# What follows on the experts' products is queued behind the cast, split and product of the chunk in front

## The chip, the core and the metric

The kernel runs on one core of one Trainium2 chip, as one launch. A core has TensorE for matrix products (PE in the profile, its weight loads PEld), VectorE (DVE), ScalarE (ACT) and GpSimd (POOL) for everything else, and SyncE (SP), which here issues most of the transfers. Each engine works through its own list of instructions in a fixed order and waits, where an instruction needs another engine's result or a buffer that is still in use, on a semaphore. The metric is the device time of one execution in microseconds. The times shown here are three runs and one profiled execution.

## The reference

One layer of an encoder on 512 tokens of 1024 numbers: a convolution module and a state-space mixer side by side, then a mixture of 32 experts of which each token takes 4, then a final norm. The change lies in the experts:

```python
gu = xb @ w_gu[e] + b_gu[e]                 # 1024 -> 2048
gate, up = jnp.split(gu, 2, axis=-1)
gate = jnp.minimum(gate, SWIGLU_LIMIT)
up = jnp.clip(up, -SWIGLU_LIMIT, SWIGLU_LIMIT)
glu = gate * jax.nn.sigmoid(SWIGLU_ALPHA * gate)
return ((up + 1.0) * glu) @ w_down[e] + b_down[e]   # 1024 -> 1024
...
out = jax.ops.segment_sum(ys * buf_w[:, None], buf_tok, num_segments=t + 1)[:t]
```

All numbers are float32. An expert's weights are 12 MB, and all 32 experts' are read once.

## The kernel before

The first 880 us or so compute the mixer, the convolution and the routing. From then on the experts follow one another in steps. A step has one block of tokens, up to 128 (a large expert, `three3`) or up to 64 (a small one, `two2`); from step 2 on large and small take turns, and two steps (11 and 21) have a second, small block for the same expert.

The weights come in **chunks** of 1 MB, 384 in all, numbered `n` in the order in which they are used: 8 for the gate and up product (`gu`, 128 of the 1024 rows each) and 4 for the down product (`dn`, 256 rows each). In most steps (`mixed`) the down chunks of the expert before are put between the gate and up chunks of this one. Every chunk goes through the same stations:

- SP loads it into one of `NRAW` = 7 raw buffers (`mr`, `m_load`).
- ScalarE casts it to fp32r, the high part (`mh`, line 1352), VectorE takes what the cast lost, the low part (`ml`, line 1353, the split); both are written by `m_split` into one of `NHL` = 4 slots. The raw buffer is free when the split is done.
- TensorE multiplies (`m_product`): with a large block 12 products of 512 columns a chunk (high by high, low by high, high by low), with a small one 8. The slots of `mh` and `ml` are free when they are done.

In the loop over chunks `m_load(n + 6)`, `m_split(n + 3)` and `m_product(n)` are written one after the other. On the products follow, by name:

- `lower` (ScalarE, `bgu` and `bdn`, line 1450) copies the lower 64 rows of a small block's result, which hold the products with the tokens' low part,, and `folded` (TensorE, line 1453) adds them to the upper 64; `bias` (line 1436) adds a large block's bias.
- `act`: ScalarE's `sg` (line 1415) and VectorE's two operations on `h` (1416, 1417).
- `h_parts`: TensorE transposes `h` (`trh`, line 1385), ScalarE and VectorE split it into `hh` and `hl` (1395, 1396); the down products read both.
- `leave`: VectorE scales the result into `y` (line 1427), and `scatter` adds it to the output with an indirect transfer of GpSimd (line 1431).
- `gather` (line 1366) fetches the next tokens with an indirect transfer, and `x_parts` transposes and splits them (`trx`, `xh`, `xl`; 1385, 1392, 1393).

For a small block some of this is put into the list `late`, which the loop works off behind the next chunk's product. The order of the instructions on an engine is not the order of this text: a scheduler lays them out when the kernel is built, by its own estimate of when each could start, and an instruction that it thinks ready early is put ahead of others that are written before it. `tc.issue_after(i)` is the means to bind it: instructions traced under it stay behind `i` on `i`'s engine.

After the last chunk come two loops that run only if an expert has more tokens than its blocks hold (here they are branched over), then the final norm, which reads the sum from `y_d`.

Of the kernel before, what the change touches and what calls it, by code (L numbers as in the profile page):

```python
# [2 lines left out]

# [5 lines left out]
F32 = mybir.dt.float32  # L9
# [12 lines left out]
D = 1024  # L22
KT = D // P
# [6 lines left out]
NE = 32  # L30
# [10 lines left out]
def encoder_layer_kernel(ctx: ExitStack, tc: tile.TileContext, a, out):  # L41
# [160 lines left out]
    for k in range(KT):  # L202
        pt = bank("mm", f"xT{k}")
# [1095 lines left out]
    def mixed(s):  # L1299

        return 0 < s < NE - 1 and len(steps[s]) == len(steps[s - 1]) == 1
# [41 lines left out]
    ms = mw2 = None  # L1343
    slot = {}

    def m_split(n):
        if n >= len(chunks):
            return
        raw = raws.pop(n)
        hi = mh.tile([P, 2 * DFF], F32R, tag="hi", bufs=NHL, name=f"mh{n}")  # L1350
        lo = mh.tile([P, 2 * DFF], F32R, tag="lo", bufs=NHL, name=f"ml{n}")
        S.copy(hi, raw)  # L1352
        V.tensor_sub(lo, raw, hi.bitcast(F32))  # L1353
        hls[n] = (hi, lo)

    order = [b for st_ in steps for b in st_]
# [42 lines left out]
    def x_parts(s):  # L1399
        if s < NE:  # L1400
            for b in steps[s]:
                if b in small:
                    slot[b]["fold"] = f_ = folds[small_at.index(b) % 2 if b < NE else 2]
                    G.tensor_copy(f_[:HB, :HB], selb[:, b:b + 1].bitcast(F32).to_broadcast([H2, HB]))  # L1404
                slot[b]["xT"] = two_parts(slot[b]["x"], "x", b)
# [3 lines left out]
    def act(b, gate, up, c0, n):  # L1409
        q, r = slot[b], rows(b)  # L1410
        if "h" not in q:
            q["h"] = ms.tile([P, DFF], F32, tag="hy", bufs=3, name=f"h{b}")[r]
        sg = ms.tile([P, DFF], F32, tag="sg", bufs=1, name=f"sg{b}")[r, c0:c0 + n]
        h = q["h"][:, c0:c0 + n]
        S.activation(sg, gate[r], AF.Silu, scale=ALPHA)
        V.tensor_scalar(h, up[r], LIMIT + 1.0, 1.0 - LIMIT, ALU.min, ALU.max)  # L1416
        V.scalar_tensor_tensor(h, sg, SILU_LIMIT, h, ALU.min, ALU.mult)
# [5 lines left out]
    def leave(b, cols, pd):  # L1423
        q, r = slot[b], rows(b)
        if "y" not in q:
            q["y"] = ms.tile([P, D], F32, tag="hy", bufs=3, name=f"y{b}")[r]
        V.scalar_tensor_tensor(q["y"][:, cols], pd[r], q["w"], tl["g2"][r, cols], ALU.mult, ALU.mult)  # L1427
# [10 lines left out]
    def three3(pt, l, r, k, w, cols, first):  # L1438
        PE.matmul(pt, l[:, k, :], w[0][:, cols], start=first, stop=False)  # L1439
        PE.matmul(pt, r[:, k, :], w[0][:, cols], start=False, stop=False)  # L1440
        PE.matmul(pt, l[:, k, :], w[1][:, cols], start=False, stop=False)  # L1441

    def two2(pt, l, k, w, cols, first):
        PE.matmul(pt, l[:, k, :], w[0][:, cols], start=first, stop=False)  # L1444
        PE.matmul(pt, l[:, k, :], w[1][:, cols], start=False, stop=(k == KT - 1))  # L1445

    def lower(pt, tab):
        S.copy(tab[HB:], pt[HB:])  # L1450
# [25 lines left out]
    def out_small(b, pt, cols, last):  # L1476
        for c0 in range(cols.start, cols.stop, T):
            folded(pt[:, c0 - cols.start:c0 - cols.start + T], b, bdn[:, c0:c0 + T])
            leave(b, slice(c0, c0 + T), pt[:, c0 - cols.start:c0 - cols.start + T])
        if last:  # L1480
            scatter(b)

    def m_product(n, kind, blocks, k):
        w = hls.pop(n)
        b = blocks[0]
        if kind == "gu" and len(blocks) == 1:
            if k == 0:
                pend["gu"] = [banks(f"gu{i}", b) for i in range(2)]
            gate, up = (flat(x) for x in pend["gu"])
            for j in range(4):  # L1490
                cs, pt = slice(j * T, (j + 1) * T), pend["gu"][j // 2][:, j % 2, :]
                parts(b, "xT", k, pt, w, cs, k == 0)
                if k == KT - 1 and b not in small:
                    bias(pt, b, bgu, cs)
            if k == KT - 1:
                if b in small:
                    lower(gate, bgu[:, 0:D])
                    lower(up, bgu[:, D:])
                    late.append(lambda: act_small(b, gate, up, None))
                else:  # L1500
                    act(b, gate, up, 0, D)
        elif kind == "gu":
            n_, kp = divmod(k, 4)
            if kp == 0:
                pend["gu"] = [banks(tag, b_) for tag, b_ in zip(("dn", "gu0") if n_ else ("gu0", "gu1"), blocks)]
            for kk in range(2):
                for i, b_ in enumerate(blocks):
                    for h in range(2):
                        cs = slice(kk * D + h * T, kk * D + (h + 1) * T)
                        parts(b_, "xT", 2 * kp + kk, pend["gu"][i][:, h, :], w, cs, kp == 0 and kk == 0)  # L1510
            if kp == 3:
                cols = slice(n_ * T, (n_ + 1) * T)
                (g1_, u1_), (g2_, u2_) = ([x[:, h, :] for h in range(2)] for x in pend["gu"])
                for h, pt in enumerate((g1_, u1_)):
                    bias(pt, b, bgu, slice(h * D + n_ * T, h * D + (n_ + 1) * T))
                act(b, g1_, u1_, n_ * T, T)
                for h, pt in enumerate((g2_, u2_)):
                    lower(pt, bgu[:, h * D + n_ * T:h * D + (n_ + 1) * T])
                late.append(lambda: act_small(blocks[1], g2_, u2_, cols))
        elif len(blocks) == 1:  # L1520
            if k == 0:
                pend["dn"] = banks("gu0" if b == NE - 1 else "dn", b)
            for kk in range(2):
                for j in range(2):
                    cs = slice(kk * D + j * T, kk * D + (j + 1) * T)
                    parts(b, "hT", 2 * k + kk, pend["dn"][:, j, :], w, cs, k == 0 and kk == 0)
            if k == 3:
                pt = flat(pend["dn"])
                if b in small:
                    lower(pt, bdn)  # L1530
                    out_small(b, pt, slice(0, D), True)
                else:
                    for j in range(2):
                        cs = slice(j * T, (j + 1) * T)
                        bias(pt[:, cs], b, bdn, cs)
                        leave(b, cs, pt[:, cs])
                    scatter(b)
        else:
            n_, kq = divmod(k, 2)
            if kq == 0:  # L1540
                pend["dn"] = banks("gu1" if n_ else "dn", b)
            for kk in range(4):
                for i, b_ in enumerate(blocks):
                    parts(b_, "hT", 4 * kq + kk, pend["dn"][:, i, :], w, slice(kk * T, (kk + 1) * T), kq == 0 and kk == 0)
            if kq == 1:
                cs, (p1_, p2_) = slice(n_ * T, (n_ + 1) * T), [pend["dn"][:, i, :] for i in range(2)]
                bias(p1_, b, bdn, cs)
                leave(b, cs, p1_)
                if n_:
                    scatter(b)  # L1550
                lower(p2_, bdn[:, cs])
                late.append(lambda: out_small(blocks[1], p2_, cs, n_ == 1))

    tlw.close()
    mw2 = moe.enter_context(tc.tile_pool(name="mw2", bufs=1, reuse_waits="tile"))
# [54 lines left out]
    for n, (kind, s, k) in enumerate(chunks):  # L1610
        if n:
            m_load(n + NRAW - 1)
        if n == 3 * KT:
            n_rest = nc.values_load(ovr[0:1, 2 * NOVR:2 * NOVR + 1], min_val=0, max_val=NOVR)
            n_any = nc.values_load(ovr[0:1, 2 * NOVR + 1:2 * NOVR + 2], min_val=0, max_val=1)
        if n == len(chunks) - 4:
            with tc.issue_after(last_load[0].ins):
                final_rows()
        m_split(n + NHL - 1)
        now, late[:] = list(late), []  # L1620
        m_product(n, kind, steps[s], k)
        for f_ in now:
            f_()
        if s == 0 and kind == "gu" and k < KT - 1:
            next(placing, None)
            if k >= KT - 1 - len(biases):
                bias_table(*biases[k - KT + 1 + len(biases)])
        if kind == "gu" and k == (4 if s == 0 else 6 if mixed(s) else KT - 1):
            x_parts(s + 1)
        if kind == "gu" and k == KT - 1:  # L1630
            gather(s + 2)
        if kind == "gu" and s > 0 and k == 1:
            h_parts(steps[s - 1])
        if kind == "dn" and s == NE - 2 and k == 3:
            h_parts(steps[s + 1])

    V.scalar_tensor_tensor(tl["gf"], tl["gf"], 1.0, tl["g_"], ALU.add, ALU.mult)


# [78 lines left out]
```

## Time and profile before

| | |
|---|---|
| runs | 2109.12, 2112.2, 2113.71 us; median 2112.2 |
| the profiled execution's own time | 2111.7 us |
| its span, first to last instruction | 2110.0 us |
| PE, PEld busy | 1908.0 us (90%), 1458.8 us (69%) |
| DVE, ACT, POOL busy | 1728.4 us (82%), 1336.9 us (63%), 686.5 us (33%) |
| DMA | 548.52 MB, mean 260 GB/s |
| a chunk's cast, a chunk's split | 1905 ns, 2282 ns, 384 of each |
| a 1 MB load, issue to landing | 7.7 us (median) |

Busy shares are a mean over parts of the kernel that have different limits; what matters here is the stretch from 950 us on, where the experts are. A busy TensorE is not one at its peak: a product that waits for an operand after it has begun counts as busy. "A <- B" in a row of waits means that the instruction A stood at the head of its engine's list and B ended its wait. Chunk numbers are not in the trace; they are in the orders of instructions shown with the change, as the number behind `mh`, `ml` and `mr`.

### The profile page before, as it was taken

To read this page: it belongs to the slowest core of one execution; us is meant where nothing else is said; L and a number is where in the kernel's file an instruction comes from. 1 tells how busy PE (TensorE), PEld (TensorE's weight loads), DVE (VectorE), ACT (ScalarE), POOL (GpSimd) and SP (SyncE) were. 2 spreads that over 40 slices of the span, in tenths; PEclk is the share of its full clock that TensorE was granted. 3 is DMA by queue.
4 is the path that set the end of the run, shared out by engine and by line. 5 is a ranking of instruction groups with operands and counts; after the bars stand their busy time and mean duration, and the time that the engine had idled before them with its cause. 6 is when DMAs were issued, how large, how long until landed. Compare 5 with 4: busy or idle time off the path is not lost.

```text
span 2110.0 us, 24644 instructions
## 1 busy us (share of the span) xinstructions
PE 1908.0 (90%) x8412; PEld 1458.8 (69%) x8412; DVE 1728.4 (82%) x1646; ACT 1336.9 (63%) x1556; POOL 686.5 (33%) x387
## 2 busy tenths in 40 slices
PE   5998999989997999799999899999989999989983
PEld 4776777767776778677667667776666777766662
DVE  7878888989857555699989887888988888898895
ACT  4657567576746223367677775776777677677773
POOL 2166364565654232321122132132212312321103
PEclk8999999999998999799999999999999999999996
DMA  8443313224366867589999999899999989999993
GB/s 265 120 138 94 89 55 85 72 64 123 102 203 192 265 207 248 175 313 384 360 360 371 371 336 352 325 350 366 354 364 351 345 319 348 367 353 351 356 374 131
DMA packets 232643, 548.52 MB, mean 260 GB/s; under 512 B 18006, under 2 KB 124766, under 8 KB 201789
## 3 DMA queue, kind: packets, MB, share of 16 engines
q1 hardware_dynamic: 224258, 529.01, 69.8%
q0 software_dynamic: 8208, 17.89, 3.7%
q8 instruction: 68, 1.11, 0.2%
q14 instruction: 61, 0.50, 0.1%
q10 hardware_dynamic: 48, 0.01, 0.0%
HBM read 526.37 MB, written 29.91 MB: 264 GB/s over the span
## 4 chain that ended last, share of the span: by engine, by line
PE 39%; DVE 11%; issue 8%; ACT 3%; DMA 1%; POOL 1%; another core or an unknown queue 0%; POOLq 0%; DVEq 0%; SPq 0%; ACTq 0%
DVE ml L1353 8%; PE gu L1439 6%; PE gu L1441 6%; PE gu L1440 5%; PE gu L1444 3%; PE gu L1445 3%; PE dn L1445 3%; PE dn L1441 2%; PE dn L1444 2%; PE dn L1440 2%; PE dn L1439 2%; ACT mh L1352 1%; PE gu L1436 1%; ACT bgu L1450 1%; DVE hl L1396 1%
## 5 line engine op out<-in xcount | busy, mean ns | idle before, releaser
L1353 DVE TENSOR_TENSOR ml<-mr,mh 128x2048 fp32r<-128x2048 f32 x384 | 861.9, 2282 | 71.6 <-ACT mh L1352 71.2
L1352 ACT CAST mh<-mr 128x2048 fp32r<-128x2048 f32 x384 | 711.9, 1905 | 95.2 <-PE gu L1444 41.9
L1431 POOL DMA_INDIRECT y_d<-y,toks_b x32 | 125.2, 3913 | 373.6 <-DVE y L1427 351.8
L1445 PE MATMUL gu<-ml,xh 128*128 128x512 f32 x576 | 215.4, 402 | 28.9 <-DVE ml L1353 27.7
L1444 PE MATMUL gu<-mh,xh 128*128 128x512 f32 x576 | 209.3, 392 | 0.0
L1439 PE MATMUL gu<-mh,xh 128*128 128x512 f32 x480 | 195.7, 408 | 1.2 <-ACT xh L1392 1.2
L1440 PE MATMUL gu<-mh,xl 128*128 128x512 f32 x480 | 189.6, 395 | 1.0 <-DVE xl L1393 1.0
L635 DVE SCALAR_TENSOR_TENSOR ha<-hb,c,ha 128x497 f32<-128x497 f32 (+14 forms) x240 | 176.8, 737 | 6.8 <-ACT ha L630 4.3
L1441 PE MATMUL gu<-ml,xh 128*128 128x512 f32 x480 | 181.8, 400 | 0.3 <-DVE ml L1353 0.2
L1366 POOL DMA_INDIRECT xg<-v_d,toks_b x32 | 116.2, 3630 | 187.2 <-PE trx L1385 180.6
L1445 PEld LDWEIGHTS gu<-ml,xh 128*128 128x128 f32 x576 | 108.1, 188 | 66.9 <-DVE ml L1353 45.2
L1404 POOL CAST fold<-selb 64x64 fp32r<-64x64 f32 x18 | 33.5, 1869 | 321.6 <-PE dn L1453 296.1
L1444 PEld LDWEIGHTS gu<-mh,xh 128*128 128x128 f32 x576 | 108.2, 188 | 21.0 <-issue 1.0
L1445 PE MATMUL dn<-ml,hh 128*128 128x512 f32 x256 | 104.8, 409 | 14.9 <-DVE ml L1353 14.9
L722 DVE SCALAR_TENSOR_TENSOR acc<-araw,cT,acc 128x512 f32<-128x512 f32 x84 | 83.3, 992 | 39.7 <-DMA araw<-in_final_ada_w_dram 22.4
L1441 PE MATMUL dn<-ml,hh 128*128 128x512 f32 x240 | 97.8, 408 | 17.8 <-DVE ml L1353 17.2
L1439 PEld LDWEIGHTS gu<-mh,xh 128*128 128x128 f32 x480 | 91.0, 190 | 30.6 <-issue 11.5
L1441 PEld LDWEIGHTS gu<-ml,xh 128*128 128x128 f32 x480 | 90.5, 190 | 23.8 <-issue 4.7
L1444 PE MATMUL dn<-mh,hh 128*128 128x512 f32 x256 | 103.9, 406 | 0.7 <-DVE h L1416 0.6
L1440 PEld LDWEIGHTS gu<-mh,xl 128*128 128x128 f32 x480 | 91.2, 190 | 19.0 <-DVE xl L1393 1.7
L1440 PE MATMUL dn<-mh,hl 128*128 128x512 f32 x240 | 93.9, 391 | 0.8 <-DVE hl L1396 0.8
L1439 PE MATMUL dn<-mh,hh 128*128 128x512 f32 x240 | 94.1, 392 | 0.0
(570 smaller groups left out, 4277.8 us busy)
## 6 DMA issues: line engine op xcount, KB each, us to landing
mr<-in_w_gu_dram SPq DMA_DIRECT2D x240, 1024.0 KB, 7.7
mr<-in_w_down_dram SPq DMA_DIRECT2D x128, 1024.0 KB, 7.8
araw<-in_ada_w_dram SPq DMA_DIRECT2D x64, 256.0 KB, 2.8
mr<-in_w_gu_dram SPq DMA_DIRECT2D x32, 512.0 KB, 9.1
ada<-in_ada_w_dram SPq DMA_DIRECT2D x32, 256.0 KB, 5.4
wX_raw<-in_w_in_dram SPq DMA_DIRECT2D x16, 512.0 KB, 3.9
wZ_raw<-in_w_in_dram SPq DMA_DIRECT2D x16, 512.0 KB, 3.8
araw<-in_final_ada_w_dram SPq DMA_DIRECT2D x32, 256.0 KB, 4.9
```

The source lines that it names most:

```text
L635: V.scalar_tensor_tensor(acc[:, lo_:hi_], h[:, lo_ + s:hi_ + s], c1[:, i, k:k + 1], acc[:, lo_:hi_], ALU.mult, ALU.add)
L722: V.scalar_tensor_tensor(acc, raw, cT[:, k:k + 1], acc, ALU.mult, ALU.add)
L1352: S.copy(hi, raw)
L1353: V.tensor_sub(lo, raw, hi.bitcast(F32))
L1366: gathered.append(nc.gpsimd.indirect_dma_start(out=x_, out_offset=None, in_=v_d, in_offset=bass.IndirectOffsetOnAxis(ap=tok_[r], axis=0), ...
L1404: G.tensor_copy(f_[:HB, :HB], selb[:, b:b + 1].bitcast(F32).to_broadcast([H2, HB]))
L1431: nc.gpsimd.indirect_dma_start(out=y_d, out_offset=bass.IndirectOffsetOnAxis(ap=q["tok"], axis=0), in_=q["y"], in_offset=None, bounds_chec ...
L1439: PE.matmul(pt, l[:, k, :], w[0][:, cols], start=first, stop=False)
L1440: PE.matmul(pt, r[:, k, :], w[0][:, cols], start=False, stop=False)
L1441: PE.matmul(pt, l[:, k, :], w[1][:, cols], start=False, stop=False)
L1444: PE.matmul(pt, l[:, k, :], w[0][:, cols], start=first, stop=False)
L1445: PE.matmul(pt, l[:, k, :], w[1][:, cols], start=False, stop=(k == KT - 1))
```

## The change

`m_split` and the products write down their last cast, split and matmul in `last_of`. The context `queued()` binds what is traced in it behind these three, each on its engine. Under it stand now: `lower` and `act` at the end of a gate and up product, `lower` and `leave` at the end of a down product, what `late` holds, and `x_parts`, `gather` and `h_parts` in the loop. GpSimd's and SP's instructions have no entry in `last_of`. Beside this `out_small` of a small expert's only block goes into `late` instead of being called at once; `out_small` of a two-block step's last half is called at once instead of going into `late`; and what is left in `late` after the loop is worked off there.

```diff
+    last_of = {}
+
+    @contextmanager
+    def queued():
+
+        with ExitStack() as st_:
+            for i in last_of.values():
+                st_.enter_context(tc.issue_after(i.ins))
+            yield
...
-        S.copy(hi, raw)
-        V.tensor_sub(lo, raw, hi.bitcast(F32))
+        last_of["ACT"] = S.copy(hi, raw)
+        last_of["DVE"] = V.tensor_sub(lo, raw, hi.bitcast(F32))
...
-        PE.matmul(pt, l[:, k, :], w[1][:, cols], start=False, stop=False)
+        last_of["PE"] = PE.matmul(pt, l[:, k, :], w[1][:, cols], start=False, stop=False)
...
-                    lower(gate, bgu[:, 0:D])
-                    lower(up, bgu[:, D:])
+                    with queued():
+                        lower(gate, bgu[:, 0:D])
+                        lower(up, bgu[:, D:])
                     late.append(lambda: act_small(b, gate, up, None))
                 else:
-                    act(b, gate, up, 0, D)
+                    with queued():
+                        act(b, gate, up, 0, D)
...
                 if b in small:
-                    lower(pt, bdn)
-                    out_small(b, pt, slice(0, D), True)
+                    with queued():
+                        lower(pt, bdn)
+                    late.append(lambda: out_small(b, pt, slice(0, D), True))
...
-                        leave(b, cs, pt[:, cs])
+                        with queued():
+                            leave(b, cs, pt[:, cs])
...
-                late.append(lambda: out_small(blocks[1], p2_, cs, n_ == 1))
+                if n_:
+                    out_small(blocks[1], p2_, cs, True)
+                else:
+                    late.append(lambda: out_small(blocks[1], p2_, cs, False))
...
         m_product(n, kind, steps[s], k)
-        for f_ in now:
-            f_()
+        with queued():
+            for f_ in now:
+                f_()
...
+        with queued():
+            if kind == "gu" and k == (4 if s == 0 else 6 if mixed(s) else KT - 1):
+                x_parts(s + 1)
+            if kind == "gu" and k == KT - 1:
+                gather(s + 2)
+            if kind == "gu" and s > 0 and k == 1:
+                h_parts(steps[s - 1])
+            if kind == "dn" and s == NE - 2 and k == 3:
+                h_parts(steps[s + 1])
+
+    for f_ in late:
+        f_()
+    late.clear()
```

How the instructions stand now, at three places. In the rows, `mh89` and `ml89` are cast and split of chunk 89. Chunk 89 is the last gate and up chunk of expert 7 (large); 90 and 91 are the last down chunks of expert 6 (small); 92 to 95 belong to the gate and up product of expert 8 (small), and 96 is the first down chunk of expert 7.

ScalarE around the end of expert 7's gate and up product, before:

```order
L1352 CAST mh89_9499<-mr89_9437 128x2048
L1352 CAST mh90_9517<-mr90_9455 128x2048
L1415 ACTIVATE sg7_9583<-gu0_7_9375 128x1024
L1352 CAST mh91_9531<-mr91_9470 128x2048
L1352 CAST mh92_9562<-mr92_9497 128x2048
L1450 CAST bdn_7587<-dn_6_9461 64x1024
L1352 CAST mh93_9592<-mr93_9515 128x2048
L1395 ACTIVATE hh_9666<-trh_9657 128x1024
L1352 CAST mh94_9606<-mr94_9529 128x2048
```

And after:

```order
L1363 CAST mh89_9499<-mr89_9437 128x2048
L1363 CAST mh90_9517<-mr90_9455 128x2048
L1363 CAST mh91_9531<-mr91_9470 128x2048
L1403 CAST xh_9557<-trx_9548 128x8x64
L1363 CAST mh92_9562<-mr92_9497 128x2048
L1426 ACTIVATE sg7_9583<-gu0_7_9375 128x1024
L1363 CAST mh93_9592<-mr93_9515 128x2048
L1363 CAST mh94_9606<-mr94_9529 128x2048
L1461 CAST bdn_7587<-dn_6_9461 64x1024
L1363 CAST mh95_9621<-mr95_9560 128x2048
L1363 CAST mh96_9645<-mr96_9590 128x2048
L1406 ACTIVATE hh_9666<-trh_9657 128x1024
```

`sg7`, which needs product 89, stood behind the cast of chunk 90 and stands behind that of chunk 92; `bdn` of expert 6, which needs product 91, moves from behind cast 92 to behind cast 94; `hh` of expert 7 from behind cast 93 to behind cast 96. The cast of expert 8's tokens `xh`, which is ahead of these rows in the order before (behind cast 85), stands between casts 91 and 92.

VectorE at the same place, before:

```order
L1353 TENSOR_TENSOR ml90_9518<-mr90_9455,mh90_9517 128x2048
L1416 TENSOR_SCALAR h7_9582<-gu1_7_9376 128x1024
L1353 TENSOR_TENSOR ml91_9532<-mr91_9470,mh91_9531 128x2048
L1417 SCALAR_TENSOR_TENSOR h7_9582<-sg7_9583,h7_9582 128x1024
L1353 TENSOR_TENSOR ml92_9563<-mr92_9497,mh92_9562 128x2048
L1427 SCALAR_TENSOR_TENSOR y6_9620<-dn_6_9461,w_b_6784,row_g2_6810 64x512
L1353 TENSOR_TENSOR ml93_9593<-mr93_9515,mh93_9592 128x2048
L1427 SCALAR_TENSOR_TENSOR y6_9620<-dn_6_9461,w_b_6784,row_g2_6810 64x512
L1396 SCALAR_TENSOR_TENSOR hl_9667<-trh_9657,hh_9666 128x1024
```

And after:

```order
L1364 TENSOR_TENSOR ml91_9532<-mr91_9470,mh91_9531 128x2048
L1404 TENSOR_TENSOR xh_9557<-trx_9548,xh_9557 128x8x64
L1364 TENSOR_TENSOR ml92_9563<-mr92_9497,mh92_9562 128x2048
L1427 TENSOR_SCALAR h7_9582<-gu1_7_9376 128x1024
L1364 TENSOR_TENSOR ml93_9593<-mr93_9515,mh93_9592 128x2048
L1428 SCALAR_TENSOR_TENSOR h7_9582<-sg7_9583,h7_9582 128x1024
L1364 TENSOR_TENSOR ml94_9607<-mr94_9529,mh94_9606 128x2048
L1364 TENSOR_TENSOR ml95_9622<-mr95_9560,mh95_9621 128x2048
L1438 SCALAR_TENSOR_TENSOR y6_9636<-dn_6_9461,w_b_6784,row_g2_6810 64x512
L1364 TENSOR_TENSOR ml96_9646<-mr96_9590,mh96_9645 128x2048
L1438 SCALAR_TENSOR_TENSOR y6_9636<-dn_6_9461,w_b_6784,row_g2_6810 64x512
L1407 SCALAR_TENSOR_TENSOR hl_9667<-trh_9657,hh_9666 128x1024
```

The two operations on `h7` stood behind splits 90 and 91 and stand behind splits 92 and 93; the second `y6` and `hl` of expert 7 stood behind split 93 and stand behind split 96.

VectorE at the end of the last down product (chunks 380 to 383, expert 31, small; `xg1` with `gfin` is a table of the final norm), before:

```order
L1353 TENSOR_TENSOR ml380_15877<-mr380_15820,mh380_15876 128x2048
L1427 SCALAR_TENSOR_TENSOR y30_15914<-dn_30_15856,w_b_6784,row_g2_6810 64x512 x2
L1353 TENSOR_TENSOR ml381_15889<-mr381_15834,mh381_15888 128x2048
L1353 TENSOR_TENSOR ml382_15901<-mr382_15850,mh382_15900 128x2048
L1353 TENSOR_TENSOR ml383_15938<-mr383_15874,mh383_15937 128x2048
L1637 SCALAR_TENSOR_TENSOR xg1_7492<-xg1_7492,gfin_15935 128x1024
L1427 SCALAR_TENSOR_TENSOR y31_15976<-gu0_31_15941,w_b_6784,row_g2_6810 64x512
```

And after:

```order
L1364 TENSOR_TENSOR ml381_15889<-mr381_15834,mh381_15888 128x2048
L1364 TENSOR_TENSOR ml382_15901<-mr382_15850,mh382_15900 128x2048
L1407 SCALAR_TENSOR_TENSOR hh_15922<-trh_15913,hh_15922 128x8x64
L1364 TENSOR_TENSOR ml383_15930<-mr383_15874,mh383_15929 128x2048
L1660 SCALAR_TENSOR_TENSOR xg1_7492<-xg1_7492,gfin_15927 128x1024
L1438 SCALAR_TENSOR_TENSOR y30_15943<-dn_30_15856,w_b_6784,row_g2_6810 64x512 x2
L1438 SCALAR_TENSOR_TENSOR y31_15976<-gu0_31_15933,w_b_6784,row_g2_6810 64x512
```

The two `y30` stood behind split 380 and stand behind split 383 and the table; the split of `h31` into `hh` stands ahead of split 383 and was ahead of split 380 before.

## Rows read from the trace of the kernel before

**Rows 1.** Busy time by stretch of the experts' part. Columns: the stretch (us from the span's start) and its length; busy us (and count) of PE, PEld, DVE, ACT and POOL; the granted TensorE clock; the DMA engines' busy share; GB/s. The stretches are cut where `sg` of a large expert begins; the last one ends with the `bgu` of expert 31.

```profile
953.60:1019.71 66.11, 66.11 (x295) 51.09 (x295) 61.32 (x35) 47.82 (x31) 9.67 (x4) 1.00 1.00 382
1019.71:1091.75 72.04, 66.71 (x285) 48.75 (x285) 64.09 (x36) 51.62 (x33) 15.21 (x5) 1.00 0.97 367
1091.75:1164.19 72.44, 67.05 (x285) 48.75 (x285) 64.09 (x36) 51.65 (x33) 15.24 (x5) 1.00 0.98 364
1164.19:1236.60 72.41, 66.40 (x285) 48.89 (x285) 64.10 (x36) 51.74 (x33) 14.11 (x5) 1.00 0.97 367
1236.60:1301.63 65.03, 59.94 (x260) 44.48 (x261) 55.36 (x32) 46.67 (x30) 27.44 (x5) 1.00 0.98 351
1301.63:1400.22 98.59, 95.74 (x426) 75.33 (x424) 81.78 (x51) 67.84 (x50) 16.88 (x8) 0.97 0.85 315
1400.22:1467.64 67.42, 65.38 (x287) 49.33 (x287) 61.24 (x36) 48.39 (x32) 25.98 (x6) 1.00 1.00 374
1467.64:1539.97 72.33, 66.30 (x285) 48.91 (x285) 64.09 (x36) 51.79 (x33) 14.10 (x5) 1.00 0.97 363
1539.97:1612.43 72.46, 66.46 (x285) 48.88 (x285) 64.09 (x36) 51.78 (x33) 14.13 (x5) 1.00 0.96 365
1612.43:1677.50 65.07, 60.01 (x260) 44.48 (x261) 55.36 (x32) 46.68 (x31) 27.46 (x5) 1.00 0.98 354
...
1775.69:1843.21 67.52, 65.50 (x287) 49.32 (x287) 61.23 (x36) 48.39 (x32) 25.96 (x6) 1.00 1.00 372
1843.21:1915.63 72.42, 66.43 (x285) 48.90 (x285) 64.09 (x36) 51.84 (x33) 14.12 (x5) 1.00 0.96 359
1915.63:1988.03 72.40, 66.41 (x285) 48.90 (x285) 64.09 (x36) 51.77 (x33) 12.98 (x4) 1.00 0.96 358
1988.03:2050.09 62.06, 55.22 (x228) 38.72 (x229) 57.22 (x33) 47.14 (x30) 7.09 (x3) 1.00 0.94 354
```

**Rows 2.** Who waited for whom in one of these stretches, 1164.19 to 1236.60 us: engine, name and line of the waiting instruction, what it waited for, us in total, times, longest.

```profile
ACT sg L1415 <- PE gu L1436: 5.1, 1, 5.1
ACT hh L1395 <- PE trh L1385: 4.6, 1, 4.6
ACT bgu L1450 <- PE gu L1445: 4.2, 1, 4.2
...
DVE h L1416 <- PE gu L1436: 3.3, 1, 3.3
...
ACT xh L1392 <- PE trx L1385: 3.1, 2, 2.3
ACT bdn L1450 <- PE dn L1445: 3.0, 1, 3.0
DVE ml L1353 <- ACT mh L1352: 2.7, 3, 1.1
PE gu L1445 <- DVE ml L1353: 2.5, 2, 1.5
PE dn L1441 <- DVE ml L1353: 2.0, 2, 1.2
DVE h L1416 <- ACT bgu L1450: 1.8, 1, 1.8
...
PE dn L1445 <- DVE ml L1353: 1.3, 1, 1.3
...
DVE y L1427 <- PE dn L1453: 0.2, 1, 0.2
DVE xh L1393 <- ACT xh L1392: 0.2, 1, 0.2
```

**Rows 3.** VectorE's groups of instructions in the same stretch: line, engine, operation, tiles, shapes, count | busy us, mean ns of one | idle us before them and what ended it.

```profile
L1353 DVE TENSOR_TENSOR ml<-mr,mh 128x2048 fp32r<-128x2048 f32 x24 | 53.7, 2283 | 2.7 <-ACT mh L1352 2.7
L1427 DVE SCALAR_TENSOR_TENSOR y<-dn,w_b,row_g 64x512 f32<-64x512 f32 (+1 forms) x4 | 3.0, 740 | 0.2 <-PE dn L1453 0.2
...
L1396 DVE SCALAR_TENSOR_TENSOR hl<-trh,hh 128x1024 fp32r<-128x1024 f32 x1 | 1.2, 1209 | 0.0
```

**Rows 4.** The same of ScalarE: the casts.

```profile
L1352 ACT CAST mh<-mr 128x2048 fp32r<-128x2048 f32 x24 | 44.2, 1903 | 0.7 <-PE dn L1440 0.7
```

**Rows 5.** The same of TensorE, shapes kept apart: the transposes of a large expert's `h`, and the small expert's folded products.

```profile
L1385 PE MATMUL trh<-ident,h 128*128 128x128 f32 x8 | 1.2, 272 | 0.0
...
L1453 PE MATMUL dn<-bdn,fold 128*128 128x512 f32 x2 | 0.9, 451 | 0.0
```

**Rows 6.** The tail. First VectorE's instructions in order of time (start us, us, engine, line, operation, tiles, shapes; in brackets the idle time before and what ended it), then two pieces of the chain that ended last (start us, us, what): the scatters of `y30` and `y31`, and what lies at the branch between them.

```profile
2067.43 6.68 DVE L1353 TENSOR_TENSOR ml<-mr,mh 128x2048 fp32r<-128x2048 f32 x3
2074.03 1.21 DVE L1637 SCALAR_TENSOR_TENSOR xg<-xg,gfin 128x1024 f32<-128x1024 f32 x1
```

```profile
2067.78 11.30 DMA y_d<-y,toks_b
...
2079.32 1.86 another core or an unknown queue
...
2084.66 3.56 DMA y_d<-y,toks_b
```

**Rows 7.** Two windows of 4 us inside a stretch, columns as in rows 1.

```profile
1104.00:1108.00 4.00, 2.60 (x10) 1.88 (x11) 4.00 (x4) 4.00 (x3) 3.16 (x2) 1.00 0.79 286
...
1124.00:1128.00 4.00, 3.94 (x18) 2.79 (x16) 3.33 (x2) 1.68 (x2) 0.00 (x0) 1.00 1.01 424
```

More of the change, by code (lines that the diff above doesn't have):

```diff
@@ L1 @@
 import math
-from contextlib import ExitStack
+from contextlib import ExitStack, contextmanager
 import concourse.bass as bass
@@ L1440, in three3 @@
         PE.matmul(pt, r[:, k, :], w[0][:, cols], start=False, stop=False)
-        PE.matmul(pt, l[:, k, :], w[1][:, cols], start=False, stop=False)
+        last_of["PE"] = PE.matmul(pt, l[:, k, :], w[1][:, cols], start=False, stop=False)
     def two2(pt, l, k, w, cols, first):
         PE.matmul(pt, l[:, k, :], w[0][:, cols], start=first, stop=False)
-        PE.matmul(pt, l[:, k, :], w[1][:, cols], start=False, stop=(k == KT - 1))
+        last_of["PE"] = PE.matmul(pt, l[:, k, :], w[1][:, cols], start=False, stop=(k == KT - 1))
     def lower(pt, tab):
@@ L1627, in encoder_layer_kernel @@
                 bias_table(*biases[k - KT + 1 + len(biases)])
[L1628 to L1635, printed above, removed]
+        with queued():
[10 more added lines that the diff above has]
+    late.clear()
     V.scalar_tensor_tensor(tl["gf"], tl["gf"], 1.0, tl["g_"], ALU.add, ALU.mult)
```

## The prediction

> **What bounds the kernel now.** I read the busy table first, then the last 1100 us by stage, then the waits of one repeating stretch, then its durations, then the tail.
>
> The experts' part runs from about 950 to 2076 us. An expert's weights come as 12 chunks of 1 MB; a "pair" below is 24 chunks, one large expert's step and one small one's, cut where `sg` of the large expert begins. Seven pairs repeat almost exactly: 72.04, 72.44, 72.41, 72.33, 72.46, 72.42 and 72.40 us, 506.5 in all [rows 1]. In none of them is an engine full: VectorE is busy for 64.1 us of the 72.4, ScalarE for 51.7. TensorE's 66 to 67 is swollen by waiting inside matmuls; its need follows from the first stretch, where it never idles and puts 295 records into 66.11 us, 0.2241 us each, so 285 records need 63.9 us. The DMA engines are busy for a share of 0.96 to 0.98. So three resources lie within 13% of each other and none sets the time alone. Yet three stretches of the same 24 chunks ran in 66.11, 67.42 and 67.52 us, at 372 to 382 GB/s and a DMA share of 1.00 [rows 1]: the ones after the start and after each two-block step, when TensorE had been the slow one and casts and splits had run ahead to their four slots. What is lost later is that lead.
>
> The waits of one pair say how [rows 2]. ScalarE stands for 20.0 us (5.1 + 4.6 + 4.2 + 3.1 + 3.0) and each time the instruction at its head is a follow-up of a product (`sg`, `hh`, `bgu`, `xh`, `bdn`) that waits for TensorE; casts stand behind it. VectorE stands idle for 8.3 us (72.4 - 64.1; its rows are 3.3 + 2.7 + 1.8 + 0.2 + 0.2), and TensorE then waits 5.8 us for splits (2.5 + 2.0 + 1.3). No row has a cast waiting for a load, so loads are not late yet.
>
> **The change, part by part.** No instruction, byte or buffer is added; the order on three engines moves.
>
> *Follow-ups behind the cast and split of chunk n + 3.* Casts have four slots, so the cast of chunk n + 4 needs the slot that product n frees. A follow-up of product n that stands right behind cast n + 3 waits for the same event as the next cast: its wait is free. In the order before, `sg7` (it needs product 89) stands behind cast 90, ahead of casts 91 and 92, whose slots were free one and two products earlier; now it stands behind cast 92. `bdn` moves from behind cast 92 to behind 94. On VectorE the first operation of `h7` moves from behind split 90 to behind 92. These are the rows of 5.1 and 3.0 us on ScalarE and of 3.3 us on VectorE [rows 2]. `xh` moves with its transposes: in the old order TensorE transposes four or more chunks earlier in the step than the text of the loop asks and ScalarE waits for that; now they stand behind product 88, and `xh` is ready well before product 92. I expect most of VectorE's 8.3 us to go, and with it the 5.8 us on TensorE.
>
> *What is late next.* Not TensorE (63.9 us) nor VectorE (64.1), but the loads: the seven pairs' share, 0.967 on average, gives 506.5 x 0.967 = 489.8 us. A second way: each of the seven rows' GB/s by its time is 25.9 to 26.6 MB, 184.0 MB in all; at 376 GB/s, the mean of the three full stretches, they take 489.4 us [rows 1]. Both give about 17 us, 2.4 a pair, and a pair of 69.9. That is the main term: **-17 us**. Its ends: at 382 GB/s 481.7 us, so -25; and nothing gained, if the share is already the ceiling.
>
> *The down product's low part is later.* `hl7` stood behind split 93 and now stands behind split 96 and the second `y6`. Counted from the end of product 92 (it frees the slot of cast 96): TensorE's way to the first matmul that reads `hl7` is 7 matmuls of chunk 93, 8 transposes (1.2 us), a fold (0.45), chunks 94 and 95 (16 matmuls) with a second fold in them, and 3 matmuls: 26 x 0.224 + 1.2 + 0.9 = 7.9 us. VectorE's way is cast 1.90 and split 2.28, then the second `y6`, which needs the second fold (21 of the 26 matmuls and the rest: 6.8), 0.74, and `hl7`, 1.21: 8.8 us [rows 3, 4, 5]. So TensorE waits 0.9 us. The split itself has 6.8 - 4.2 = 2.6 us to spare; if two more splits (4.56) stood in front of it, the wait would be 0.9 + 2.0 = 2.9. It lies under the loads (63.9 + 2.9 is below 69.9): I charge nothing; if loads were no bound, it would cost 0.9 to 2.9 a pair, 6 to 20 in all.
>
> *Other stretches.* The two stretches of 18 chunks (65.03 and 65.07 us, share 0.98) can give 1.3 each, the last one (62.06, share 0.94, but VectorE 57.2) up to 3.7; I take 1, 1 and 2: **-4 us**. The two-block steps have TensorE busy for 95.74 of 98.59 us, and the three full stretches have the loads at 1.00 [rows 1]: nothing there.
>
> *The tail.* The small expert's output is now deferred, and at the end `y30` moves from behind split 380 to behind split 383 and `gf`. Its scatter started at 2067.78 us and landed 11.30 us later; the branch into the loop behind it waits for that landing [rows 6]. `gf` ends at 2075.2 (2074.03 + 1.21); two `y` of 0.74 later, 2076.7, the scatter can start. With VectorE quiet the next scatter took 3.56 us from issue to landing, with VectorE busy 11.30. So the landing comes at 2080.3 or 2088.0 instead of 2079.1: +1.2 to +9. No split is left then, so I take the near end: **+1.5 us**.
>
> *Costed at nothing.* GpSimd's instructions keep their order. A gather waits for the transposes that free its buffer, so it starts later by the chunks that `xh` moved, but its rows are wanted a step or more after; it decides only if that reserve goes. SP's loads keep theirs; some register reads between them move, at the moments when SP waits for splits anyway.
>
> The sum is -17 - 4 + 1.5 = -19.5 us against the profiled execution's own 2111.7 us (span 2110.0): 2092.2. That execution lies 0.5 us under the median of the three runs, 2112.2, so I predict **2093**.
>
> The Trainium skill's page "DMA: Bandwidth & Descriptors" (section "Specifications") puts HBM at about 358 GB/s per core; by it pairs at 358 to 367 GB/s are at the ceiling and the main term is zero. The trace disagrees with it here: whole pairs ran at 372 to 382 [rows 1]. The same page's "Measured" section has 425 GB/s for one core with long transfers; by that, as an estimate, the 184.0 MB would take 433 us and VectorE would be the bound.
>
> **The rivals.**
> *The loads are the ceiling already.* A share of 0.96 to 0.98 with unequal packets may be all there is: of the windows of 4 us one moved 286 GB/s at a share of 0.79, another 424 at 1.01 [rows 7]. Then less waiting on ScalarE only shows as longer landing times, and pairs stay at 72. For it: the share. Against it: the 67-us pairs with the same traffic. Time: 2111.7 + 1.5 - 2 = about 2111.
> *VectorE becomes the bound.* If loads can do 184.0 MB in 7 x 64.1 = 449 us, 410 GB/s, pairs fall to 64.1: -58 - 4 + 1.5, 2051. For it: 424 GB/s in one window; against it: no pair was above 382.
> *The follow-ups become too late (slower).* The order now makes TensorE's down products wait for `hl`, `hh` and `y` behind further splits. TensorE has 72.4 - 63.9 = 8.5 us of room a pair; from there on it decides. With 5 us at both steps (two late splits, 4.6, and a little of the counted 0.9) a pair is 63.9 + 10 = 73.9, +1.5, 10.5 over the seven, and 3 for the other stretches and the tail: 2125. Against it: the count above gives 0.9 to 2.9, and at one of the two steps only.
> That the change moves nothing is excluded: the instruction orders differ.
>
> **How the numbers follow.** The forecast holds 0.62 of the chance; its own range is 2082 (382 GB/s: -25 - 6.3 + 1.5, the other stretches at all they can give) to 2104 (half of the two gains, -10.5, and 3 in the tail). VectorE's bound 0.08, loads already the ceiling 0.15, slower 0.15. No change means within 0.2%, about 4 us, which is what a measurement of this kernel can tell. Faster is 0.62 + 0.08, same 0.15, slower 0.15. The range reaches from 2072, half way to the time of VectorE's case, to 2116, all of the no-change case; what is left out is most of the slower case and half of VectorE's.
>
> **What would show it.** Right: ScalarE's waits for TensorE under 10 us a pair, VectorE's idle time under 6, DMA share 0.99 or more, pairs of 69 to 70.5, and casts that now wait for loads. Wrong in the main term: pairs still at 72 with the share up; wrong in the count of `hl`: rows of TensorE waiting for `hl` or `hh` of more than 3 us a pair; wrong in the tail: `y30`'s scatter landing later than 4 us after its issue.

## The result and the profile after

The changed kernel takes 2049.2 us (median of four runs, 2047.3 to 2051.1), the one before in the same comparison 2110.7 (2107.8 to 2113.7): a ratio of 0.9709, 95% interval 0.969 to 0.9727. That is 61 us less, where 19.5 were forecast. The profiled execution took 2048.2 us with a span of 2046.5, 63.5 less than before.

The busy time by stretch, cut as in [rows 1] (same columns):

```profile
955.64:1021.95 66.31, 66.31 (x295) 51.22 (x295) 63.68 (x38) 51.90 (x32) 10.44 (x4) 1.00 0.99 381
1021.95:1086.76 64.81, 64.12 (x285) 49.26 (x285) 64.05 (x37) 52.77 (x34) 11.58 (x5) 1.00 1.02 395
1086.76:1151.85 65.09, 64.39 (x285) 49.18 (x285) 63.40 (x36) 52.83 (x33) 10.17 (x5) 1.00 1.02 402
1151.85:1218.15 66.30, 64.98 (x286) 49.43 (x286) 63.64 (x37) 53.17 (x33) 9.04 (x5) 1.00 1.02 400
1218.15:1281.21 63.06, 59.56 (x259) 45.48 (x259) 53.45 (x32) 43.69 (x29) 25.47 (x5) 0.97 1.02 369
1281.21:1380.73 99.52, 94.20 (x426) 74.75 (x425) 80.86 (x52) 67.44 (x51) 34.87 (x8) 0.98 0.86 311
1380.73:1445.63 64.90, 64.23 (x287) 49.66 (x287) 63.94 (x37) 52.70 (x34) 12.27 (x5) 1.00 1.02 397
1445.63:1510.36 64.73, 64.07 (x285) 49.25 (x285) 63.74 (x37) 52.80 (x33) 12.07 (x5) 1.00 1.02 399
1510.36:1575.86 65.50, 64.81 (x286) 49.37 (x286) 63.34 (x36) 52.88 (x33) 10.92 (x6) 1.00 1.02 401
1575.86:1637.31 61.45, 58.16 (x259) 44.42 (x260) 53.35 (x32) 43.81 (x29) 25.31 (x5) 1.00 1.02 374
1637.31:1737.49 100.18, 95.30 (x426) 75.53 (x425) 80.94 (x52) 67.51 (x51) 35.30 (x7) 0.97 0.85 306
1737.49:1802.39 64.90, 64.23 (x287) 49.67 (x287) 63.95 (x37) 52.69 (x33) 12.29 (x5) 1.00 1.01 393
1802.39:1867.19 64.80, 64.13 (x285) 49.26 (x285) 64.14 (x37) 52.76 (x33) 11.60 (x5) 1.00 1.02 400
1867.19:1932.28 65.09, 64.40 (x285) 49.18 (x285) 63.97 (x37) 52.86 (x33) 9.10 (x4) 1.00 1.02 396
```

The seven repeating pairs (rows 2 to 4, 8, 9, 13 and 14) now take 64.7 to 66.3 us, 456.3 in all, against 506.5: -50.2. Row by row, the two 24-chunk stretches behind the two-block steps give -5.1 more, the two of 18 chunks -5.6, the two-block steps +2.9, the start and the first stretch +2.2. What follows the last large `sg` gives -7.8 (2046.5 - 1932.28 against 2110.0 - 1988.03). The sum is -63.6; the spans differ by 63.5, the rest is rounding.

In a steady pair TensorE is busy for 64.1 us of 64.8, VectorE for about 63.3 to 64.1, and the DMA engines show a share of 1.02 at 395 to 402 GB/s. The waits of one such pair, 1086.76 to 1151.85 us, to be held against [rows 2]:

```profile
ACT mh L1363 <- DMA mr<-in_w_down_dram: 4.9, 4, 2.0
ACT mh L1363 <- PE gu L1451: 2.2, 4, 0.8
ACT mh L1363 <- PE dn L1451: 1.4, 1, 1.4
ACT mh L1363 <- PE dn L1455: 1.4, 2, 0.8
...
ACT hh L1406 <- PE trh L1396: 1.0, 1, 1.0
DVE ml L1364 <- ACT mh L1363: 0.9, 3, 0.4
...
ACT sg L1426 <- PE gu L1447: 0.7, 1, 0.7
ACT sg L1426 <- PE gu L1464: 0.7, 1, 0.7
...
DVE h L1427 <- PE gu L1447: 0.6, 1, 0.6
PEld dn L1451 <- DVE hl L1407: 0.5, 1, 0.5
...
PE dn L1450 <- DVE y L1438: 0.5, 1, 0.5
```

The 20.0 us in which ScalarE stood at a follow-up have shrunk to 2.4 (1.0 + 0.7 + 0.7). What it waits for now are slots, which a product must free before a cast can write (5.0 us: 2.2 + 1.4 + 1.4), and, for the first time in a pair, loads (4.9). TensorE's 5.8 us of waiting for splits are gone from the rows. The seven pairs are not alike in this: follow-ups cost ScalarE 1.4 to 4.7 us, slots and follow-ups together 6.0 to 11.9, and loads 0 to 7.2. In the pair of 64.80 us from 1802.39 on, at 400 GB/s, no cast waits for a load; in the longest, 66.30 us, casts wait 7.2.

### The profile page after: what moved, and what is told of

Read it like the earlier page. It is cut to its first block, busy times and chain, and to the rows that moved or that the text cites. A ratio compares the mean times of both kernels' runs of the same rounds, so it can differ in the third digit from the quotient of the medians.

```text
span 2046.5 us, 24604 instructions
## 1 busy us (share of the span) xinstructions
PE 1886.9 (92%) x8412; PEld 1467.0 (72%) x8412; DVE 1726.6 (84%) x1646; ACT 1348.3 (66%) x1556; POOL 667.2 (33%) x387
## 3 DMA queue, kind: packets, MB, share of 16 engines
q1 hardware_dynamic: 224258, 529.01, 70.5%
## 4 chain that ended last, share of the span: by engine, by line
PE 39%; DVE 8%; issue 6%; DMA 5%; ACT 3%; POOL 1%; another core or an unknown queue 0%; POOLq 0%; DVEq 0%; ACTq 0%; SPq 0%
PE gu L1450 5%; DVE ml L1364 5%; PE gu L1452 5%; PE gu L1451 5%; PE gu L1455 4%; PE gu L1456 4%; DMA mr<-in_w_down_dram 3%; PE dn L1452 3%; PE dn L1451 2%; PE dn L1450 2%; PE dn L1455 2%; PE dn L1456 2%; ACT mh L1363 2%; PE gu L1447 1%; DMA mr<-in_w_gu_dram 1%
## 5 line engine op out<-in xcount | busy, mean ns | idle before, releaser
L1363 ACT CAST mh<-mr 128x2048 fp32r<-128x2048 f32 x384 | 722.9, 1906 | 202.4 <-PE gu L1455 53.4
L1442 POOL DMA_INDIRECT y_d<-y,toks_b x32 | 153.3, 4789 | 234.2 <-DVE y L1438 212.4
L1455 PE MATMUL gu<-mh,xh 128*128 128x512 f32 x576 | 212.7, 395 | 0.0
L1377 POOL DMA_INDIRECT xg<-v_d,toks_b x32 | 92.5, 2891 | 346.8 <-PE trx L1396 338.9
L1450 PE MATMUL gu<-mh,xh 128*128 128x512 f32 x480 | 196.7, 411 | 5.9 <-ACT sg L1426 4.7
L1456 PE MATMUL dn<-ml,hh 128*128 128x512 f32 x256 | 101.9, 398 | 0.4 <-DVE ml L1364 0.3
L1452 PE MATMUL dn<-ml,hh 128*128 128x512 f32 x240 | 95.1, 396 | 0.9
L1415 POOL CAST fold<-selb 64x64 fp32r<-64x64 f32 x18 | 8.1, 455 | 259.0 <-PE dn L1464 234.1
```

Source lines behind the costliest of these rows:

```text
L1363: last_of["ACT"] = S.copy(hi, raw)
L1377: gathered.append(nc.gpsimd.indirect_dma_start(out=x_, out_offset=None, in_=v_d, in_offset=bass.IndirectOffsetOnAxis(ap=tok_[r], axis=0), ...
L1442: nc.gpsimd.indirect_dma_start(out=y_d, out_offset=bass.IndirectOffsetOnAxis(ap=q["tok"], axis=0), in_=q["y"], in_offset=None, bounds_chec ...
L1452: last_of["PE"] = PE.matmul(pt, l[:, k, :], w[1][:, cols], start=False, stop=False)
L1456: last_of["PE"] = PE.matmul(pt, l[:, k, :], w[1][:, cols], start=False, stop=(k == KT - 1))
```

## The experiments

Theory A at the start: the time of before sat in waits at the head of ScalarE's list, with ready casts behind them; without them TensorE (63.9 us a pair) and VectorE (64.1) bind, and the loads have room. Rivals: the loads are a ceiling (B); the gain is TensorE's or VectorE's order (C); the three queues gain only together (D).

**One engine at a time.** `queued` keeps the binding to only one of the three (cast, split or matmul); for the fourth run it keeps none, so that only the deferred output of the small experts is left of the change.

```diff
-            for i in last_of.values():
-                st_.enter_context(tc.issue_after(i.ins))
+            for e_ in ("ACT",):
+                if e_ in last_of:
+                    st_.enter_context(tc.issue_after(last_of[e_].ins))
```

> Follow-ups queue behind the newest cast on ScalarE alone; nothing holds them back on VectorE and TensorE. Theory A (the time sat in ScalarE's head-of-line waits, 20.0 us of a 72.4 us pair, and their removal lets TensorE reach its 63.9 us): most of the gain, 2050 to 2065 us. Rival C (the gain comes from VectorE's or TensorE's order): 2095 to 2111 us. Rival D (the three queues gain only together): 2095 us or more, with waits that have moved from ScalarE to VectorE or TensorE.

> Follow-ups queue behind the newest split on VectorE alone. Theory A: VectorE's idle in a pair of before was 8.3 us and its casts still come late from ScalarE, so at most a third of the gain: 2090 to 2111 us. Rival C: 2049 to 2065 us.

> Follow-ups (transposes and folds) queue behind the newest product on TensorE alone. Theory A: 2100 to 2115 us, since TensorE waited for splits. Rival C in its TensorE form: 2049 to 2080 us.

> The deferral of the small experts' outputs by one product stays, the queueing behind cast, split and product goes on all three engines. Theory A: the time of before, 2105 to 2113 us. If the deferral is what gained: 2049 to 2080 us.

ScalarE alone: 0.9985 (0.9965 to 1.0004). VectorE alone: 1.0151 (1.0122 to 1.0181), slower. TensorE alone: 0.998 (0.9966 to 0.9995). None: 1.0004 (0.9992 to 1.0016). So the deferral gains nothing, and theory A falls in its simple form: ScalarE's order alone gives nothing, though in the pair shown here its list of instructions is, one by one, that of the changed kernel. Its waits say why. First the waits of one pair of the run with ScalarE alone (columns as in [rows 2]), then VectorE's instructions in order of time (start us, us, instruction; idle before and what ended it) at one place:

```profile
DVE h L1428 <- PE gu L1448: 5.8, 1, 5.8
...
PEld gu L1457 <- DVE ml L1365: 3.0, 4, 1.2
PEld dn L1452 <- DVE hl L1408: 2.1, 1, 2.1
PEld gu L1451 <- DVE h L1428: 1.8, 1, 1.8
...
ACT bdn L1462 <- PE dn L1457: 1.7, 1, 1.7
ACT hh L1407 <- PE trh L1397: 1.7, 1, 1.7
```

```profile
1082.93 4.48 DVE L1365 TENSOR_TENSOR ml<-mr,mh 128x2048 fp32r<-128x2048 f32 x2
1093.20 1.22 DVE L1428 TENSOR_SCALAR h<-gu 128x1024 f32<-128x1024 f32 x1 [5.79 <-PE gu L1448]
1094.34 2.28 DVE L1365 TENSOR_TENSOR ml<-mr,mh 128x2048 fp32r<-128x2048 f32 x1
```

ScalarE stands at `sg` for 1.2 us where it stood 5.1, but VectorE stands 5.8 us at `h`, and behind it is a split whose cast is done. The wait has changed engines (3.3 us in [rows 2]). A limit of these runs: where one engine's queueing is left out, the scheduler also places some instructions of the other engines otherwise. With VectorE alone a pair has VectorE waiting 11.1 us for casts, and ScalarE standing 7.2 us at `xh`, 3.2 at `sg` and 2.5 at `bdn`; why that is slower than before isn't settled.

**Two engines.** The revised theory: a product needs a cast and then a split, so a wait at the head of either list stops both.

```diff
+            for e_ in ("ACT", "DVE"):     # e6: ("ACT", "PE")
```

> Follow-ups queue behind cast and split on ScalarE and VectorE, nothing holds them back on TensorE. Theory A is revised after the three runs with one engine each: a product needs its cast and its split in turn, so a wait at the head of either queue stops both, and freeing one moves the wait to the other (VectorE's h on up waited 60.8 us for TensorE in 12 places in the run with ScalarE alone). Revised theory A: both engines together give most of the gain, pairs 65 to 67 us, 2050 to 2070 us. Rival D (TensorE's queueing is needed as well, since its transposes and folds wait at its head): 2085 us or more, with TensorE's waits for xh, hh or h at over 3 us a pair.

> Follow-ups queue behind cast and product on ScalarE and TensorE, nothing holds them back on VectorE. Revised theory A: VectorE's waits at its head remain, 2090 to 2111 us. Rival E (TensorE's and ScalarE's order are what counts, VectorE has slack): 2050 to 2070 us.

ScalarE with VectorE: 2047.9 us, 0.9697 (0.9666 to 0.9728), the whole gain. ScalarE with TensorE: 0.9992 (0.9975 to 1.0009), nothing, with VectorE's `h` waiting 11.5 us in two pairs. The revised theory holds, though the time lies 2 us under its range; D and E (TensorE's queueing is needed as well; VectorE's isn't) fall. TensorE's queueing alone is worth 0.2%, and beside the other two nothing that these intervals show. A pair with ScalarE and VectorE queued, by stretch; both lists in it are those of the changed kernel:

```profile
1085.33:1150.29 64.96, 64.37 (x285) 49.29 (x285) 62.61 (x36) 52.94 (x34) 16.10 (x5) 1.00 1.02 398
```

**Which follow-ups.** In `e11` the two blocks in the loop are no longer queued, in `e12` those inside `m_product`.

```diff
-        with queued():          # e11: the loop's two; e12: m_product's four
+        if 1:
```

> Only the follow-ups that stand inside a product (sg and h of large experts, the casts that lower small ones, the y of large ones) queue behind cast, split and product; the deferred ones, x parts and h parts do not. Revised theory A: waits at the heads remain for xh, hh and the small experts' sg, and one that remains holds both queues: 2070 to 2105 us. Rival F (the follow-ups inside the product alone cost the time): 2049 to 2065 us.

> The other half: the deferred follow-ups, x parts and h parts queue behind cast, split and product; those inside a product do not. Revised theory A: waits at the heads remain for the large experts' sg and for the lowering casts: 2070 to 2105 us, and the gains of the two halves are together about 61 us or less. Rival F: 2095 to 2111 us.

Those inside the product alone: 0.9882 (0.9857 to 0.9908), 2085.3 us, as expected, with pairs of 68.6 and ScalarE waiting for `xh` (6.3 us) and `hh` (6.0). The deferred ones alone: 1.0114 (1.0091 to 1.0136), slower, against my expectation; ScalarE stands 6.6 us a pair at `sg` and 5.0 at `bgu`, VectorE 4.9 at `h`. So the two halves (-25 and +26 us) don't add up to the whole's -61: what one half frees, the heads that are left take back. F (the follow-ups inside the product alone cost the time) falls.

**Work and loads.** First less work for the two busy engines (where no low part is formed, the product takes the high part in its place), then half the bytes:

```diff
 # e7
-        PE.matmul(pt, r[:, k, :], w[0][:, cols], start=False, stop=False)
-        last_of["PE"] = PE.matmul(pt, l[:, k, :], w[1][:, cols], start=False, stop=False)
+        last_of["PE"] = PE.matmul(pt, r[:, k, :], w[0][:, cols], start=False, stop=False)
...
-        last_of["DVE"] = V.tensor_sub(lo, raw, hi.bitcast(F32))
+        last_of["DVE"] = V.tensor_sub(lo[:, :3 * T], raw[:, :3 * T], hi[:, :3 * T].bitcast(F32))
 # e8
-            last_load[0] = dma.dma_start(raw, wg[k * P:(k + 1) * P, :])
+            h_ = 2 * DFF if n < NRAW else DFF
+            last_load[0] = dma.dma_start(raw[:, :h_], wg[k * P:(k + 1) * P, :h_])
...
+            raw = raw[:, None, :DFF].to_broadcast([P, 2, DFF])
```

> The changed kernel; large experts leave out their third product (48 of 285 matmuls of a pair, -10.8 us at 0.224), and VectorE forms the low part of three quarters of each chunk's columns (24 splits of 2.28 us shorten by about 0.55, -13 us). Theory A (TensorE 63.9 and VectorE 64.1 bind a pair, the loads have room): pairs fall to 55 to 62 us, loads at 405 to 455 GB/s, 1930 to 2010 us. Rival B (loads at 395 to 402 GB/s are the ceiling): pairs stay 63 to 65 us, 2030 to 2050 us.

> The changed kernel; from the eighth chunk on, a load brings half of a chunk's columns and both halves of cast and split read it, so instructions and their sizes stay. Theory A: loads don't bind, pairs stay 64 to 65 us, 2040 to 2050 us. Rival B: pairs fall below 63 us, under 2030 us.

> The changed kernel; no third product in large experts, a low part for half of the columns, and half of a chunk loaded. The run with less work had pairs of 67 to 69.5 us at 392 to 397 GB/s. If the loads held it there: pairs fall to 54 to 59 us, where ScalarE (52.9) is next. If TensorE's lower clock (0.92 to 0.95) or its order held it: pairs stay above 63 us.

Half the loads: 0.9675 (0.9651 to 0.97), pairs as in the changed kernel. Less work: 0.9516 (0.9486 to 0.9547), but the pairs do not fall to 55 to 62 us, they take 65 to 70; what it gains lies in the two-block steps (142 and 144 us with their 18-chunk stretches, against 163 and 162) and ahead of the first 24-chunk stretch, which begins 20 us sooner. Both together: 0.8709 (0.8688 to 0.8729), with pairs a little under the expected 54 us. By stretch, one pair of half loads, then one of less work and its stretch behind the first two-block step, then one of both:

```profile
1085.50:1150.68 65.18, 64.05 (x285) 49.28 (x286) 63.74 (x37) 52.58 (x34) 12.21 (x6) 1.00 0.71 213
```

```profile
1072.35:1139.41 67.06, 59.42 (x236) 42.77 (x236) 51.86 (x36) 52.87 (x35) 9.79 (x5) 0.92 1.01 392
```

```profile
1349.12:1413.96 64.84, 59.10 (x256) 43.40 (x255) 51.83 (x37) 52.65 (x34) 8.74 (x5) 1.00 1.02 403
```

```profile
1042.38:1095.73 53.35, 52.32 (x237) 40.43 (x237) 39.75 (x36) 51.75 (x35) 7.62 (x5) 1.00 0.83 262
```

The waits of ScalarE in that pair of less work:

```profile
ACT mh L1363 <- DMA mr<-in_w_down_dram: 6.1, 7, 2.2
ACT mh L1363 <- DMA mr<-in_w_gu_dram: 4.3, 6, 1.5
```

With 213 GB/s instead of 400 a pair is no shorter: in the changed kernel the loads don't set it, TensorE and VectorE do. (The 18-chunk stretches do gain by it: 59.8 us each, for 63.1 and 61.5.) But with those two relieved by about 11 us (48 x 0.224) and 12 us (64 - 51.9) it isn't shorter either: no engine is full, casts wait 10.4 us for loads, and 391 to 404 GB/s is what comes in the stretches of 24 chunks. The lower clock of that pair (0.92) isn't what holds them: another pair at 0.92 took 65.28 us, the stretch at 1.00 took 64.84, both at 402 to 403 GB/s. Relieved on all three sides a pair falls to 53.4, with TensorE busy for 52.3 of it and ScalarE for 51.8; no row has a cast waiting for a load. That third run takes more work off VectorE too (39.8 us for 51.9), but VectorE was not full in the second, and ScalarE's list in a pair is the same in both. So the loads have a ceiling, as B said, but it lies at the rate that the changed kernel has just reached: three resources end within 2% of each other. Whether the DMA engines or the seven raw buffers set this ceiling, no run tells.

**Before's order with half the loads.** Did the heads of the lists set the 72.4 us of before, or the loads?

> The kernel before; from the eighth chunk on, a load brings half of a chunk's columns and both halves of cast and split read it. Revised theory A (waits at the heads of ScalarE's and VectorE's queues set a pair of before): pairs stay 71 to 72.5 us, 2090 to 2111 us. Rival B (the loads, at a share of 0.97, set it): pairs below 69 us, under 2075 us.

It took 2044.3 us, 0.9686 (0.9653 to 0.9719), against theory A and as B expected. But the order of its instructions isn't that of before. The same place of ScalarE's list, first of before, then with half loads:

```
L1352 CAST mh66_9015<-mr66_8953 128x2048
L1415 ACTIVATE sg5_9081<-gu0_5_8873 128x1024
L1352 CAST mh67_9029<-mr67_8968 128x2048
L1352 CAST mh68_9060<-mr68_8995 128x2048
```

```
L1355 CAST mh66_9015<-mr66_8953 128x2048
L1355 CAST mh67_9029<-mr67_8968 128x2048
L1355 CAST mh68_9060<-mr68_8995 128x2048
L1395 CAST xh_9055<-trx_9046 128x8x64
L1418 ACTIVATE sg5_9081<-gu0_5_8873 128x1024
```

With smaller loads the scheduler put `sg5` two casts later by itself, where the change puts it. The run changed two things and tells nothing apart. So I forced one order of before's kind on both: the follow-ups of product n ahead of cast and split n + 2, where before had the large experts' `sg`, with full and with half loads.

```diff
+    def m_split(n):
+        with ExitStack() as st_:
+            for i in foll.values():         # the latest follow-up on ACT and on DVE
+                st_.enter_context(tc.issue_after(i.ins))
+            m_split_(n)
+        foll.clear()
...
-        m_split(n + NHL - 1)
...
+        m_split(n + NHL - 2)                # behind the product and its follow-ups
```

> The kernel before, its order forced: the cast and split of chunk n+2 are issued behind the follow-ups of product n on ScalarE and VectorE (where before had the large experts' sg). Revised theory A: the time of before or a little above, pairs 71 to 76 us, 2095 to 2150 us. If the order does not matter and the loads set before's time: 2040 to 2111 us with ScalarE waiting for loads.

> The same forced order, with half of each chunk loaded from the eighth on. Revised theory A: within 1% of the run with full loads, pairs 70 to 76 us, with ScalarE and VectorE waiting for TensorE at sg, h, hh and the lowering casts. Rival B (loads set before's time): pairs below 68 us, under 2070 us.

2151.4 us with full loads, 1.0192 (1.0175 to 1.0209), 1 us above the expected range, and 2147.5 with half, 1.0168 (1.015 to 1.0185). A pair with full loads, its waits (the row of `sg` holds the waits at both ends of the pair, so 5.1 a pair), and a pair with half:

```profile
1095.46:1167.90 72.44, 67.72 (x285) 49.90 (x285) 64.10 (x36) 51.75 (x34) 29.11 (x5) 0.98 0.96 367
```

```profile
ACT sg L1424 <- PE gu L1445: 10.1, 2, 5.1
...
ACT hh L1404 <- PE trh L1394: 5.5, 2, 4.2
ACT bgu L1459 <- PE gu L1454: 4.3, 1, 4.3
DVE h L1425 <- PE gu L1445: 3.3, 1, 3.3
```

```profile
1098.40:1170.35 71.95, 67.07 (x285) 50.12 (x286) 64.19 (x37) 52.00 (x34) 28.59 (x5) 0.98 0.63 192
```

The forced order brings back the 72.4 us of [rows 1] with the waits of [rows 2], and half the loads take 0.5 us off it. The two lists still differ in one thing: with half the loads `xh` stands four or five casts later, and ScalarE waits there (6.2 us) instead of at `sg`. So an order of before's kind, with waits at the heads, is enough for a pair of 72 us, whether the loads bring 367 or 192 GB/s. (The forced kernel is slower than before elsewhere: its two-block steps, with the stretch ahead of them, take 174 to 175 us instead of 163 to 164.)

## Why the prediction was wrong

**The mechanism was right.** Follow-ups behind the newest cast and split wait for the same event as the next cast, and the heads of the lists come free: ScalarE's waits for TensorE are 7.4 us in the pair shown (2.4 + 5.0; forecast under 10), though 10.0 to 11.9 in three of the seven; VectorE's idle time is 0.7 to 2.7 us a pair (under 6), the share is 1.02, and in six of the seven pairs casts wait for loads. The pairs themselves, forecast at 69 to 70.5 us, take 64.7 to 66.3. The prediction set both engines side by side; the runs show that they gain only together.

**The step that failed is "What is late next": the loads.** I took 376 GB/s, at most 382, as what the loads can do, from the three stretches with a share of 1.00 in [rows 1], and so -17 us for the seven pairs, -25 at best. Measured: 395 to 402 GB/s in those pairs and -50.2 us. The rate of a stretch was read as its limit, where it was the result of its time: the first of the three is full of TensorE (66.11 of 66.11), and it is again after the change (66.31 of 66.31, at 381 GB/s); the other two fell to 64.90 us, at 397 and 393 GB/s. Nor is a share of 1.00 an end: it goes to 1.02 with 20 GB/s more. (The needs of TensorE, VectorE and the loads in a pair of before were 63.9, 64.1 and 70.0 us, within 10% of each other; the 13% of the prediction is the smallest one's distance from the 72.4.) The Trainium skill's page "DMA: Bandwidth & Descriptors" (section "Specifications") has about 358 GB/s per core, a stack's rate divided by two cores, by which there was no gain to be had; this kernel's one core moved up to 402 in whole pairs. Its section "Measured" has 425 GB/s for one core's long transfers; here, with casts waiting for loads in the run with less work, 391 to 404 came.

**The rival of 2051 us has the time**, but partly by luck: its sum has -58 for the pairs (64.1 us each) and -4 for the other stretches, and measured are -50.2 and -16.2. It had VectorE as the bound; TensorE is as full, and the loads are at what they can give. I gave it 0.08 because no pair of before was above 382 GB/s, which is the same misreading again.

**The count of `hl`** forecast a wait of TensorE of 0.9 to 2.9 us a pair; the row says 0.5. `y` and `sg` cost it as little in the pair shown: in the pairs the slower rival did not happen.

**Other stretches** were put at -4. The 18-chunk ones gave -5.6 for the forecast -2, the 24-chunk ones behind the two-block steps -5.1 for 0 (the same mis-sized rate), the two-block steps +2.9 for 0: in each of these TensorE now waits 3.5 us for VectorE's `h`, where it waited 0 and 0.6 before, which is the slower rival's kind of wait in the place that was put at nothing. The row of the first, 1281.21 to 1380.73 us:

```profile
PE dn L1455 <- DVE h L1427: 3.5, 1, 3.5
```

From the last large `sg` to the end of `gf` it is 76.6 us (2008.9 - 1932.28) against 87.2 (2075.2 - 1988.03): -10.6, for -2.

**The tail** was put at +1.5. From `gf` to the end it is now 37.6 us (2046.5 - 2008.9) against 34.8 (2110.0 - 2075.2): +2.8. The landing came as forecast; the chain that ended last has

```profile
2012.42 3.59 DMA y_d<-y,toks_b
2016.25 1.86 another core or an unknown queue
```

3.59 us for 3.56. But the scatter starts 3.5 us after `gf`, not 1.5, because `y30` waits for TensorE's two folds. TensorE's instructions in order of time, then two stretches of the tail by the columns of [rows 1]:

```profile
2005.61 0.79 PE L1455 MATMUL gu<-mh,hh 128*128 128x512 f32 x1 [4.23 <-DVE hh L1407]
2006.20 0.63 PE L1456 MATMUL gu<-ml,hh 128*128 128x512 f32 x1
```

```profile
2005.60:2009.60 4.00, 3.99 (x9) 3.13 (x10) 3.29 (x2) 0.00 (x0) 0.00 (x0) 0.50 0.00 0
```

```profile
2009.60:2013.00 3.40, 3.40 (x15) 2.77 (x14) 1.49 (x2) 0.00 (x0) 0.58 (x1) 0.94 0.00 0
```

TensorE had stood idle for 4.23 us waiting for `hh`, which stands behind two splits (4.48 us) on VectorE; behind that its granted clock is 0.50, the level of 1.2 GHz, and products take 0.63 us instead of 0.39 until about 2009.6. The first of the two folds lies in that stretch, the second, which starts at 2010.97, behind it.

## What to carry to other kernels

An engine's list is walked in order, so an instruction that must wait blocks ready work behind it; put it behind the last instruction that waits for the same event, and do so on every engine of the chain (here cast and split), since freeing one alone hands the wait to the other. A transfer rate in a stretch that something else fills is no ceiling: to know a ceiling, find a stretch where an engine waits for the transfers, or relieve everything else in a run. When an experiment changes sizes, read from the traces whether the scheduler changed the order too, and force the order where it did.

## What was not expected of the hardware

The DMA engines' busy share exceeded 1 and was no measure of the room left: 1.00 stood beside 372 to 382 GB/s in [rows 1], 1.02 beside 369 in one stretch and 402 in another after the change, and in the run with half loads 0.71 beside 213 GB/s, 54% of the rate of 395 at 70% of its share.
